# Dummy matmuls before the first operands, a split first load, a shorter LayerNorm chain and a last store in two parts

## The chip, the core and the metric

The kernel runs on one core of a Trainium2 chip. The core has five engines that work side by side, each through its own list of instructions in order: TensorE (PE in the profile, with the weight loads apart as PEld), VectorE (DVE), ScalarE (ACT), GpSimd (POOL) and SyncE (SP). SP mostly starts transfers (DMA) between main memory and the on-chip memory; ACT and POOL can start some too. Engines wait for one another and for transfers through semaphores. The metric is the device time of one execution in microseconds (us); the median of several executions is compared.

## What is computed

One decoder block on x of shape 2048 x 1024, float32:

```python
proj = x @ w_in[l] + b_in[l]                      # 1024 -> 9216 columns
q, k, v, g_attn, u_lru, g_lru, gate_logits = jnp.split(proj, SPLIT_POINTS, axis=-1)
...
y_a = attn @ w_attn_proj[l]                       # dilated window attention, three groups of 8 heads
...
y_b = (h * jax.nn.silu(g_lru)) @ w_lru_proj[l]    # convolution, gated linear recurrence over positions
gates = jax.nn.sigmoid(gate_logits).reshape(B, S, N_BRANCHES, D)
merged = gates[:, :, 0] * y_a + gates[:, :, 1] * y_b
out = merged @ w_out[l] + b_out[l]
x = layer_norm(DEEPNORM_ALPHA * x + out, ln_gain[l], ln_bias[l])
```

`layer_norm` subtracts the mean of each row of 1024, multiplies by 1/sqrt(variance + 1e-5), then by a gain, and adds a bias.

## The kernel before

Every float32 matrix product is done in three matmuls: each operand is split into a high part (rounded on ScalarE by a copy, `hi_lo` and `prep_w`) and a low part (the remainder, subtracted on VectorE or GpSimd), and high x high, high x low and low x high are added up in one bank (L597).

**Stage 1** is the input projection. It goes over half the positions at a time (two chunks of 512 columns), and in each half over 36 pairs of weight tiles. Each pair after the first of a half is done with seven products of sums of blocks in place of eight; the first pair (`order is None`) does the eight plain ones, since only loaded blocks are ready. A block of x, such as B11, is four tiles of 128 x 512 (B11: first half of the features, chunk 0; B21: second half, chunk 0; B12 and B22: the same of chunk 1). One product is twelve matmuls of 512 columns: over the four tiles, three each. The first pair multiplies A11 with B11, A12 with B21, A21 with B11, A22 with B21, then the same four weights with B12 and B22. The sums of blocks that later pairs need (T1 to T4) are formed on VectorE from the raw tiles (`comb`, `comb4`, `comb_part`). The order on each engine is the order in which the program text issues the instructions (`manual_schedule`); small tables of budgets (`left`, `Ask`) decide when a chain of follow-up work may go on.

At the very start the program issues, on SP: the weight A11, the four tiles of B11, the weight A12, B21, the weights A21 and A22, B12 and B22 (L858 to L868). Each transfer is 256 KB. ACT first issues the loads of `b72` (128 x 72 values, 288 bytes a row) and `lr` (128 x 64 values, L73 and L78), which nothing needs until `consts` (L847 to L851). There are eight semaphores for transfers, given out in turn; a transfer that gets one in use waits, before it is issued, for the earlier transfer on it to land. ScalarE converts in the order A11, B11, A12, B21, A21, B12, A22, B22; VectorE makes the low parts in the same order, with `consts` between B21 and A21.

Raw tiles, converted weights and results of stage 1 share 32 slots of 2 KB a partition; `take` hands out the slot that has been free longest and `give` puts it back at the end of the list. The memory of these slots is later covered by the tiles of stage 2.

**Stage 2** is attention (L931 to L1148), **stage 3** the projections of both branches and the merge, and **stage 4** (`out_job`, L1375 to L1425) the output product with LayerNorm, for 16 tiles of 128 rows. In `out_job` the 1024 output columns come in two matmul banks of 512 (in the last tile one of 512 and two of 256, `parts`). VectorE adds them to the scaled x (L1399), takes statistics (L1402, L1405); ScalarE takes the square root (L1406); VectorE subtracts the mean and multiplies by the gain (`centre`, L1410), makes the reciprocal (L1414) and improves it by one Newton step (L1416 to L1419: r <- r * (1.5 - 0.5 * (variance + eps) * r * r)), multiplies by it and adds the bias (L1423). Each half of 512 columns is then stored; in the last tile the first half by SP, the second by ACT.

Of the kernel before, what the change touches and what calls it, by code (L numbers as in the profile page):

```python
# [8 lines left out]
F32 = mybir.dt.float32  # L9
F32R = mybir.dt.float32r  # L10
AF = mybir.ActivationFunctionType
ALU = mybir.AluOpType
# [3 lines left out]
P = 128  # L16
S = 2048
D = 1024
KT = 8
NCH = 4  # L20
CH = 512
# [10 lines left out]
def hybrid_block_kernel(ctx: ExitStack, tc: tile.TileContext, a: dict, out: bass.AP):  # L32
    nc = tc.nc
    sp, act, dve, pool, pe = nc.sync, nc.scalar, nc.vector, nc.gpsimd, nc.tensor
# [35 lines left out]
    pool.affine_select(out=mask[:, P:256], in_=mask[:, P:256], pattern=[[-1, P]],  # L70
                       compare_op=ALU.is_ge, fill=NEG, base=0, channel_multiplier=1)
    b72 = cst.tile([P, 72], F32, name="b72")
    act.dma_start(b72, a["b_in"])  # L73
    bh = cst.tile([P, 72], F32, name="bh")
    bn = cst.tile([P, 72], F32, name="bn")
    bq = cst.tile([P, 64], F32, name="bq")
    lr = cst.tile([P, 8, 8], F32, name="lr")
    act.dma_start(lr, a["lru_vec"])  # L78
    brh = cst.tile([P, 2, 8], F32, name="brh")
    sp2 = cst.tile([P, 8], F32, name="sp2")  # L80

# [42 lines left out]
    ps = stA.enter_context(tc.tile_pool(name="ps", bufs=2, space=PSUM))  # L124
# [5 lines left out]
    def take(name, dt=F32R):  # L130
        if not vacant:
            raise RuntimeError(f"no slot at {now['n']}: {[x[1].name if hasattr(x[1],'name') else x[1] for x in home.values()]} chains {len(chains)}")
        i = vacant.pop(0)
        t = sl_p.tile([P, CH], dt, tag=f"s{i}", name=name)
        home[id(t)] = (i, t)
        return t

    def give(*ts):
        for t in ts:
            vacant.append(home.pop(id(t))[0])  # L140
# [63 lines left out]
        act.activation(t[:, 0], src, AF.Copy)  # L204
        eng.tensor_tensor(out=t[:, 1], in0=src, in1=flat(t[:, 0]), op=ALU.subtract)  # L205

    def load_raw(b, c, kk, use=""):
        kx = kk + (4 if b[1] == "2" else 0)
        r = xr[use + b, kk] = take(f"x{use}{b}{c}{kk}", F32)
        sp.dma_start(r, a["xT"][:, kx, c * CH:(c + 1) * CH])  # L210

    def drop_raw(b, kk):
        give(xr.pop((b, kk)))
# [7 lines left out]
    def load_w(s, n):  # L221
        r = raw[s, n] = take(f"w{n}_{s}", F32)
        sp.dma_start(r.rearrange("p (k f) -> p k f", f=P), w_part(s, "A21" if n[0] == "S" else n))

    def w_part(s, n):

        f = plan[s][1][int(n[1]) - 1][0]
        k = 4 * (int(n[2]) - 1)
        return a["w_in"][f, :, k:k + 4, :]
# [456 lines left out]
    def keep_raw(b, c, kk):  # L686
        load_raw(b, c, kk, "c")
# [167 lines left out]

    sp2n = cst.tile([P, 8], F32, name="sp2n")
    left.update(PE=0.0, ACT=0.0, DVE=0.0, POOL=0.0)
    load_w(0, "A11")  # L858
    for kk in K4:
        keep_raw("B11", 0, kk)  # L860
    load_w(0, "A12")
    for kk in K4:
        keep_raw("B21", 0, kk)
# [433 lines left out]
    for n in range(32):  # L1297
        c, f = divmod(n, 8)
# [63 lines left out]
    def load_xr(tt):  # L1362
        XR[tt] = vx_p.tile([P, D], F32, tag="x", name=f"x{tt}", bufs=3)
        sp.dma_start(XR[tt], a["x"][tt * P:(tt + 1) * P, :])

    def split_m(tt, ks=slice(0, 8)):
        c, b = divmod(tt, 4)
        m = ME[c][:, ks, b * P:(b + 1) * P]
        if ks.start == 0:
            MS[tt] = tuple(vx_p.tile([P, 8, P], F32R, tag=t, name=f"{t}{tt}", bufs=2) for t in ("mh", "ml"))  # L1370
        mh, ml = (t[:, ks] for t in MS[tt])
        act.activation(mh, m, AF.Copy)
        dve.tensor_tensor(out=ml, in0=m, in1=flat(mh), op=ALU.subtract)  # L1373

    def out_job(tt):  # L1375
        rows = slice(tt * P, (tt + 1) * P)
        x = XR.pop(tt)
        mh, ml = MS.pop(tt)
        last = tt == 15
        parts = [slice(0, CH), slice(CH, CH + 256), slice(CH + 256, D)] if last else [slice(0, CH), slice(CH, D)]  # L1380
        zz = [fp.tile([P, CH], F32, tag="z", name=f"z{tt}{n}", bufs=3)[:, 0:hs.stop - hs.start] for n, hs in enumerate(parts)]
        for k0, k1 in ((0, 6), (6, 8)) if tt == 0 else ((0, 8),) if tt % 4 else ((0, 7), (7, 8)):
            for z, hs in zip(zz, parts):
                for k in range(k0, k1):
                    w = WO[k]
                    pe.matmul(z, mh[:, k], w[:, 0, hs], start=(k == 0), stop=False)  # L1386
                    pe.matmul(z, mh[:, k], w[:, 1, hs], start=False, stop=False)  # L1387
                    pe.matmul(z, ml[:, k], w[:, 0, hs], start=False, stop=(k == 7))  # L1388
        if tt + 1 < 16:
            load_xr(tt + 1)  # L1390
            split_m(tt + 1, slice(0, 8 if (tt + 1) % 4 else 7))
        if tt == 1:
            for fn in at1:
                fn()
        dve.scalar_tensor_tensor(out=x, in0=x, scalar=ALPHA, in1=vec[0], op0=ALU.mult, op1=ALU.add)
        st_ = cst.tile([P, 4, 6], F32, tag="st", name=f"st{tt}", bufs=2)
        n = 0
        for z, hs in zip(zz, parts):
            dve.tensor_tensor(out=x[:, hs], in0=x[:, hs], in1=z, op=ALU.add)  # L1399
            step = 256 if last else CH  # L1400
            for q in range(hs.start, hs.stop, step):
                dve.bn_stats(out=st_[:, n, :], in_=x[:, q:q + step])  # L1402
                n += 1
        mv = cst.tile([P, 4], F32, tag="mv", name=f"mv{tt}", bufs=2)
        dve.bn_aggr(out=mv[:, 0:2], in_=st_[:, 0:n])  # L1405
        act.activation(mv[:, 2:3], mv[:, 1:2], AF.Sqrt, bias=epst)  # L1406
        halves = (slice(0, CH), slice(CH, D))

        def centre(hs):
            dve.scalar_tensor_tensor(out=x[:, hs], in0=x[:, hs], scalar=mv[:, 0:1], in1=vec[1][:, hs],  # L1410
                                     op0=ALU.subtract, op1=ALU.mult)

        centre(halves[0])
        dve.reciprocal(out=mv[:, 2:3], in_=mv[:, 2:3])  # L1414

        dve.tensor_scalar(out=mv[:, 1:2], in0=mv[:, 1:2], scalar1=EPS, scalar2=-0.5, op0=ALU.add, op1=ALU.mult)  # L1416
        dve.tensor_tensor(out=mv[:, 3:4], in0=mv[:, 2:3], in1=mv[:, 2:3], op=ALU.mult)
        dve.tensor_scalar(out=mv[:, 3:4], in0=mv[:, 3:4], scalar1=mv[:, 1:2], scalar2=1.5, op0=ALU.mult, op1=ALU.add)
        dve.tensor_tensor(out=mv[:, 2:3], in0=mv[:, 2:3], in1=mv[:, 3:4], op=ALU.mult)  # L1419
        for hs, eng in zip(halves, (sp, act) if last else (act, act)):  # L1420
            if hs.start:
                centre(hs)
            dve.scalar_tensor_tensor(out=x[:, hs], in0=x[:, hs], scalar=mv[:, 2:3], in1=vec[2][:, hs],  # L1423
                                     op0=ALU.mult, op1=ALU.add)
            eng.dma_start(out[rows, hs], x[:, hs])  # L1425
# [26 lines left out]
    for tt in range(16):  # L1452
        c, b = divmod(tt, 4)
        run(late)
        out_job(tt)
        if c + 1 < NCH:
            for f in (((0, 1), (2, 3), (4, 5, 6), (7,)) if c else ((), (0, 1, 2), (3, 4, 5, 6), (7,)))[b]:
                ya_job(8 * (c + 1) + f)
            if b == 3:
                split_m(tt + 1, slice(7, 8))  # L1460
                bring_at(c + 2)
        now["n"] += 1
# [59 lines left out]
```

## Time and profile before

| | us |
|---|---|
| median of three runs (2135.4 to 2137.36) | 2137.27 |
| the profiled execution | 2143.06 |
| its span, first to last instruction | 2141.3 |
| TensorE busy | 2101.0 |
| first matmul starts | 5.75 |
| last matmul ends | 2133.2 |

The profile is of one execution, which took longer than the three timed ones. Its mean granted TensorE clock is 0.996 of full speed. A timeline row gives the start, the duration, the engine (with a q: its queue, which issues transfers), the line, the operation with output <- inputs, and in brackets how long the engine had been idle and what ended that. Such rows can merge several instructions (x3). In a table by stage the numbers behind a stretch are the busy time and count of each engine. In the names, `xcB` are raw tiles of x blocks, `xB` the converted ones, `xT` the converted sums, `wA` raw weights, `hA` and `l` their high and low parts.

### The profile page before, as it was taken

The numbers are of one execution on the slowest core, as the hardware profiler recorded it, in microseconds if no ns is written. First come the engines' busy times: TensorE is split into PE (matmuls) and PEld (weight loads), VectorE is DVE, ScalarE is ACT, GpSimd is POOL, SyncE is SP. The second block draws the span as 40 slices with busy tenths as digits, with TensorE's granted clock in tenths as the row PEclk, the third lists the DMA queues.
The fourth block names the chain that finished last, engine by engine and source line by source line (L and its number), as shares of the span: only waits on it lengthen the run. The fifth ranks groups of instructions, "written<-read, shape, count | busy, mean of one in ns | idle before, by whom it ended". The sixth has DMA issues, their size and how long they took to land.

```text
span 2141.3 us, 36029 instructions
## 1 busy us (share of the span) xinstructions
PE 2101.0 (98%) x12016; PEld 1749.0 (82%) x12016; DVE 1700.2 (79%) x3009; ACT 1080.3 (50%) x2284; POOL 736.5 (34%) x581
## 2 busy tenths in 40 slices
PE   8999999999999999999999999999999999999998
PEld 6888887888888788888888887888888888878887
DVE  8788988999979977787787886886999645466667
ACT  6354545457446565546557666557999411121100
POOL 1545454554654312121222221222535434322120
PEclk9999999999999999999999999999999999999999
DMA  8888887998998977777778788779898788874431
GB/s 269 257 261 251 255 255 224 270 280 245 286 270 251 302 228 203 227 221 218 248 244 276 254 260 253 241 229 373 303 305 254 219 275 280 283 251 160 165 108 69
DMA packets 348266, 525.74 MB, mean 246 GB/s; under 512 B 123568, under 2 KB 156336, under 8 KB 344240
## 3 DMA queue, kind: packets, MB, share of 16 engines
q1 hardware_dynamic: 330368, 491.64, 71.0%
q0 software_dynamic: 10080, 18.35, 5.4%
q10 hardware_dynamic: 7632, 13.44, 1.8%
q8 instruction: 96, 1.57, 0.3%
q14 instruction: 90, 0.74, 0.1%
HBM read 318.18 MB, written 190.45 MB: 238 GB/s over the span
## 4 chain that ended last, share of the span: by engine, by line
PE 82%; ACT 6%; DMA 5%; DVE 5%; issue 1%; SPq 1%; POOL 0%; DVEq 0%; ACTq 0%; POOLq 0%
PE q L597 59%; ACT p L991 4%; PE z L1388 3%; PE z L1386 3%; PE z L1387 3%; PE yb L1276 2%; PE yb L1277 2%; PE yb L1278 2%; PE o L1029 1%; PE ya L1354 1%; PE ya L1355 1%; PE ya L1356 1%; PE vtp L348 1%; ACT ptb L1014 1%; DMA yb_scr<-gB 1%
## 5 line engine op out<-in xcount | busy, mean ns | idle before, releaser
L597 PE MATMUL q<-xT,hS 128*128 128x512 f32 x1680 | 519.0, 390 | 0.4 <-DVE y L216 0.4
L597 PE MATMUL q<-xT,l 128*128 128x512 f32 x1120 | 436.0, 389 | 0.0
L597 PE MATMUL q<-xB,hA 128*128 128x512 f32 x1248 | 389.0, 393 | 6.0 <-ACT xB L204 5.7
L597 PEld LDWEIGHTS q<-xT,hS 128*128 128x128 f32 x1680 | 314.1, 188 | 65.4 <-issue 0.8
L597 PE MATMUL q<-xB,l 128*128 128x512 f32 x904 | 354.8, 392 | 1.9 <-DMA l<-wl_scr 1.8
L597 PEld LDWEIGHTS q<-xB,hA 128*128 128x128 f32 x1248 | 235.0, 189 | 56.1 <-ACT xB L204 5.7
L597 PEld LDWEIGHTS q<-xT,l 128*128 128x128 f32 x1120 | 210.2, 188 | 44.0
L597 PEld LDWEIGHTS q<-xB,l 128*128 128x128 f32 x904 | 171.1, 189 | 39.4 <-DMA l<-wl_scr 2.7
L216 POOL TENSOR_TENSOR S<-S,wA 128x512 f32<-128x512 f32 x35 | 45.7, 1305 | 418.9 <-DVE S L216 328.4
L216 POOL TENSOR_TENSOR sw<-sw,sin 128x512 f32<-128x512 f32 x96 | 160.7, 1679 | 72.0 <-DMA sw<-y 59.4
L261 ACT ACTIVATE hA<-wA 128x512 fp32r<-128x512 f32 x218 | 135.7, 624 | 90.3 <-DMA wA<-in_w_in_dram 43.0
L597 PE MATMUL q<-xB,hS 128*128 128x512 f32 x560 | 175.6, 395 | 3.0 <-DVE v L216 3.0
L991 ACT ACTIVATE p<-p,sta 128x256 f32<-128x256 f32 (+1 forms) x384 | 172.2, 455 | 5.9 <-DVE sta L983 5.2
L597 PE MATMUL q<-xT,hA 128*128 128x512 f32 x560 | 173.0, 390 | 1.5 <-DVE xT L205 0.9
L261 ACT ACTIVATE hS<-S 128x512 fp32r<-128x512 f32 x175 | 109.1, 623 | 99.2 <-DVE S L216 54.6
L216 POOL TENSOR_TENSOR l<-wA,hA 128x512 fp32r<-128x512 f32 x68 | 104.9, 1543 | 83.0 <-ACT hA L261 66.5
L597 PEld LDWEIGHTS q<-xB,hS 128*128 128x128 f32 x560 | 105.1, 190 | 25.0 <-issue 3.8
L597 PEld LDWEIGHTS q<-xT,hA 128*128 128x128 f32 x560 | 104.8, 188 | 24.6 <-DVE xT L205 1.3
L983 DVE CUSTOM_DVE_ANT_0 p<-s,mask 128x256 f32<-128x256 f32 (+1 forms) x384 | 118.7, 360 | 4.7 <-PE s L976 3.7
L216 DVE TENSOR_TENSOR y<-y,cos 128x512 f32<-128x512 f32 x96 | 108.8, 1139 | 14.8 <-DMA sw<-y 14.6
L1360 POOL TENSOR_TENSOR me<-gA,ybr 128x512 f32<-128x512 f32 x32 | 49.9, 1573 | 181.2 <-DVE gA L1359 119.6
L1388 PE MATMUL z<-wo,ml 128*128 128x512 f32 (+1 forms) x264 | 101.2, 383 | 0.9 <-DVE ml L1373 0.8
(201 smaller groups left out, 4423.7 us busy)
## 6 DMA issues: line engine op xcount, KB each, us to landing
wA<-in_w_in_dram SPq DMA_DIRECT2D x253, 256.0 KB, 5.0
wl_scr<-l SPq DMA_DIRECT2D x105, 512.0 KB, 4.9
l<-wl_scr SPq DMA_DIRECT2D x105, 512.0 KB, 4.8
sw<-y SPq DMA_DIRECT2D x384, 64.0 KB, 3.0
wS<-in_w_in_dram SPq DMA_DIRECT2D x70, 256.0 KB, 4.5
wS<-in_w_in_dram POOLq DMA_DIRECT2D x70, 256.0 KB, 6.3
qh_scr<-hi SPq DMA_DIRECT2D x48, 256.0 KB, 5.2
v_scr<-vs SPq DMA_DIRECT2D x48, 256.0 KB, 4.4
```

The source lines that it names most:

```text
L216: eng.tensor_tensor(out=out, in0=in0, in1=in1, op=op)
L261: act.activation(h, r, AF.Copy)
L597: pe.matmul(bank, w[:, ks], x[:, kk, xx], start=(first and i == 0), stop=(last and i == 11))
L983: dve.tensor_tensor_reduce(out=st["p", i, j][:, h, lo:256], in0=st["s", i, j // 2][h][:, j % 2, lo:256], in1=mask[:, lo:256], scale=1.0, s ...
L991: act.activation(p, p, AF.Exp, scale=-1.0, bias=s[:, h:h + 1], accum_out=s[:, 2 + h:3 + h])
L1276: pe.matmul(yb, WL[f][:, 0, k], xx[:, 0], start=(k == 0), stop=False)
L1277: pe.matmul(yb, WL[f][:, 0, k], xx[:, 1], start=False, stop=False)
L1278: pe.matmul(yb, WL[f][:, 1, k], xx[:, 0], start=False, stop=(k == 7))
L1360: pool.tensor_tensor(out=ME[c][:, f], in0=ga, in1=yb, op=ALU.add)
L1386: pe.matmul(z, mh[:, k], w[:, 0, hs], start=(k == 0), stop=False)
L1387: pe.matmul(z, mh[:, k], w[:, 1, hs], start=False, stop=False)
L1388: pe.matmul(z, ml[:, k], w[:, 0, hs], start=False, stop=(k == 7))
```

## The change

Four edits: five matmuls on a zeroed tile ahead of everything on TensorE; tiles 0 and 2 of B11 are loaded through ACT's queue, and `b72` and `lr` behind them; the Newton step in two operations in place of three; the second half of the last row tile is normalised and stored in two parts of 256 columns.

```diff
-    act.dma_start(b72, a["b_in"])
...
-    act.dma_start(lr, a["lru_vec"])
...
-    def load_raw(b, c, kk, use=""):
+    def load_raw(b, c, kk, use="", eng=sp):
         kx = kk + (4 if b[1] == "2" else 0)
         r = xr[use + b, kk] = take(f"x{use}{b}{c}{kk}", F32)
-        sp.dma_start(r, a["xT"][:, kx, c * CH:(c + 1) * CH])
+        eng.dma_start(r, a["xT"][:, kx, c * CH:(c + 1) * CH])
...
     left.update(PE=0.0, ACT=0.0, DVE=0.0, POOL=0.0)
+    warm = take("warm", F32)
+    dve.memset(warm[:, 0:256], 0.0)
+    wps = ps.tile([P, CH], F32, tag="g", name="wps", bufs=2)
+    for _ in range(5):
+        pe.matmul(wps[:, 0:256], warm[:, 0:P], warm[:, 0:256], start=True, stop=True)
+    give(warm)
     load_w(0, "A11")
     for kk in K4:
-        keep_raw("B11", 0, kk)
+        load_raw("B11", 0, kk, "c", sp if kk % 2 else act)
+    act.dma_start(b72, a["b_in"])
+    act.dma_start(lr, a["lru_vec"])
     load_w(0, "A12")
...
-        halves = (slice(0, CH), slice(CH, D))
+        halves = parts
...
-        dve.tensor_tensor(out=mv[:, 3:4], in0=mv[:, 2:3], in1=mv[:, 2:3], op=ALU.mult)
-        dve.tensor_scalar(out=mv[:, 3:4], in0=mv[:, 3:4], scalar1=mv[:, 1:2], scalar2=1.5, op0=ALU.mult, op1=ALU.add)
-        dve.tensor_tensor(out=mv[:, 2:3], in0=mv[:, 2:3], in1=mv[:, 3:4], op=ALU.mult)
-        for hs, eng in zip(halves, (sp, act) if last else (act, act)):
+        dve.scalar_tensor_tensor(out=mv[:, 3:4], in0=mv[:, 2:3], scalar=mv[:, 2:3], in1=mv[:, 1:2], op0=ALU.mult, op1=ALU.mult)
+        dve.tensor_scalar(out=mv[:, 2:3], in0=mv[:, 3:4], scalar1=1.5, scalar2=mv[:, 2:3], op0=ALU.add, op1=ALU.mult)
+        for hs, eng in zip(halves, (sp, act, sp) if last else (act, act)):
```

The dummy tile takes the first slot and gives it back, so every later tile of stage 1 lies one slot further on. The matmuls, and all other work up to LayerNorm, stand in the same order as before on every engine.

The start of SP's list before (`xcB1100` is tile 0 of B11, chunk 0; DMAHW and a digit is a transfer semaphore):

```order
L223 DMA wA11_0_226<-in_w_in_dram 128x512
L210 DMA xcB1100_228<-in_xT_dram 128x512
L210 DMA xcB1101_230<-in_xT_dram 128x512
L210 DMA xcB1102_232<-in_xT_dram 128x512
L210 DMA xcB1103_234<-in_xT_dram 128x512
L223 DMA wA12_0_236<-in_w_in_dram 128x512
L210 DMA xcB2100_238<-in_xT_dram 128x512 [waits DMAHW0_49]
L210 DMA xcB2101_240<-in_xT_dram 128x512 [waits DMAHW1_49]
```

SP issues all four tiles of B11, and B21's first tile waits for the transfer that has semaphore 0, which is `b72`. The start of ACT's list in the changed kernel:

```order
L208 DMA xcB1100_234<-in_xT_dram 128x512
L208 DMA xcB1102_238<-in_xT_dram 128x512
L865 DMA b72_193<-in_b_in_dram 128x72
L866 DMA lr_197<-in_lru_vec_dram 128x64
L259 ACT_TABLE_LOAD
L259 ACTIVATE hA11_0_274<-wA11_0_232 128x512 [waits DMAHW1_49]
L202 ACTIVATE xB11_278<-xcB1100_234 128x512 [waits DMAHW0_49]
L202 ACTIVATE xB11_278<-xcB1101_236 128x512 [waits DMAHW3_49]
```

Tiles 0 and 2 now stand at the head of ACT's list, the two small loads behind them, and semaphore 0 belongs to tile 0. The end of VectorE's list in the changed kernel, from the reciprocal of the last row tile on:

```order
L1420 RECIPROCAL mv15_22719<-mv15_22719 128x1 [waits Activation_49]
L1422 TENSOR_SCALAR mv15_22719<-mv15_22719 128x1
L1423 SCALAR_TENSOR_TENSOR mv15_22719<-mv15_22719 128x1 [waits DVE_49]
L1424 TENSOR_SCALAR mv15_22719<-mv15_22719 128x1 [waits DVE_49]
L1428 SCALAR_TENSOR_TENSOR x15_22610<-x15_22610,mv15_22719,vec2_21021 128x512 [waits DVE_49]
L1416 SCALAR_TENSOR_TENSOR x15_22610<-x15_22610,mv15_22719,vec1_21019 128x256
L1428 SCALAR_TENSOR_TENSOR x15_22610<-x15_22610,mv15_22719,vec2_21021 128x256 [waits DVE_49]
L1416 SCALAR_TENSOR_TENSOR x15_22610<-x15_22610,mv15_22719,vec1_21019 128x256
L1428 SCALAR_TENSOR_TENSOR x15_22610<-x15_22610,mv15_22719,vec2_21021 128x256 [waits DVE_49]
```

Three small operations stood between L1416 and the first multiplication before, and one pair of 512 columns where two pairs of 256 stand now.

## The prediction

> **What bounds the kernel now.** I read the page's first two parts, then the timeline of both ends, the waits of TensorE, and windows by stage.
>
> ```profile
> PE 2101.0 (98%) x12016; PEld 1749.0 (82%) x12016; DVE 1700.2 (79%) x3009; ACT 1080.3 (50%) x2284; POOL 736.5 (34%) x581
> PE 82%; ACT 6%; DMA 5%; DVE 5%; issue 1%; SPq 1%; POOL 0%; DVEq 0%; ACTq 0%; POOLq 0%
> ```
>
> TensorE is the bound: 98% busy, 82% of the chain of waits. An edit pays only if the matmuls that come after it start earlier, or if it lies behind the last one. The change touches the first 20 us and the last 3 of a span of 2141.3 us. The start, from the timeline (start, duration, engine, in brackets the idle time before and who ended it):
>
> ```profile
> 0.81 0.41 ACTq L73 DMA_DIRECT2D b<-in_b_in_dram  x1
> 1.24 1.84 SPq L210 DMA_DIRECT2D xcB<-in_xT_dram  x4
> 4.20 0.63 ACT L261 ACTIVATE hA<-wA 128x512 fp32r<-128x512 f32 x1 [1.19 <-DMA wA<-in_w_in_dram]
> 4.86 0.69 DVE L216 TENSOR_TENSOR l<-wA,hA 128x512 fp32r<-128x512 f32 x1 [3.89 <-ACT hA L261]
> 5.06 1.98 ACT L204 ACTIVATE xB<-xcB 128x512 fp32r<-128x512 f32 x3 [0.23 <-DMA xcB<-in_xT_dram]
> 5.75 1.52 PE L597 MATMUL q<-xB,hA 128*128 128x512 f32 x2 [5.75 <-ACT xB L204]
> 7.92 0.63 ACT L204 ACTIVATE xB<-xcB 128x512 fp32r<-128x512 f32 x1 [0.88 <-DMA xcB<-in_xT_dram]
> 13.28 2.66 ACT L204 ACTIVATE xB<-xcB 128x512 fp32r<-128x512 f32 x4 [0.72 <-DMA xcB<-in_xT_dram]
> 16.52 0.73 PE L597 MATMUL q<-xB,hA 128*128 128x512 f32 x2
> 16.59 0.68 DVE L216 TENSOR_TENSOR l<-wA,hA 128x512 fp32r<-128x512 f32 x1
> 17.33 0.50 PE L597 MATMUL q<-xB,l 128*128 128x512 f32 x1
> 17.59 2.50 DVE L205 TENSOR_TENSOR xB<-xcB,xB 128x512 fp32r<-128x512 f32 x4 [0.32 <-ACT xB L204]
> 48.23 0.50 PE L597 MATMUL q<-xT,hA 128*128 128x512 f32 x1 [0.91 <-DVE xT L205]
> ```
>
> The first matmul starts at 5.75. Three gates follow: block B12 (the four conversions at 13.28 wait for their loads), the rest of the fourth weight (l at 16.59, ending 17.27, for the matmul at 17.33), and at 48.23 VectorE's splits, which TensorE waits for 0.91 us. In between:
>
> ```profile
> 5.70:10.30 4.60, 4.55 (x10) 3.38 (x11) 3.75 (x6) 3.54 (x6) 0.00 (x0) 1.00 1.01 365
> 10.30:14.90 4.60, 4.60 (x21) 3.68 (x21) 4.58 (x14) 3.66 (x7) 0.00 (x0) 1.00 1.05 392
> 17.30:47.30 30.00, 29.97 (x131) 24.51 (x131) 29.36 (x45) 19.69 (x36) 5.97 (x6) 1.00 0.84 234
> ```
>
> After the stretch come busy times and counts of PE, PEld, DVE, ACT and POOL, the granted clock, DMA share and GB/s. The first 4.6 us hold 10 matmuls, the next 21 in the same time: the array begins at half pace, though the clock column says 1.00 in both. From 17.3 to 47.3 VectorE is busy 29.36 of 30.00 us: it sets when 48.23 happens. DMA moves 365 to 392 GB/s in the first two stretches: loading bounds the start.
>
> **Dummy matmuls.** They wait for a new memset of 256 columns behind one_t on VectorE, idle then until 4.86.
>
> ```profile
> 13.10 0.23 DVE L852 MEMSET ubs<- 128x200 f32 x1
> L1029 PE MATMUL o<-ptb,V 128*64 128x128 f32 x1200 | 77.1, 279 | 14.4 <-ACT ptb L1014 13.9
> 1521.60 1.97 PE L1029 MATMUL o<-ptb,V 128*64 128x128 f32 x32 [0.24 <-ACT ptb L1014]
> ```
>
> The nearest memset (200 columns) takes 0.23, so TensorE begins at about 1.3. The trace has no plain float32 matmul of 256 columns. The nearest is L1029: 600 in the program leave 1200 records, and 32 records of 128 columns take 1.97 us, 0.062 each. Five dummies are ten records of 256 columns: 1.2 us at full pace, 2.5 at half; twice that, 4.9, if the two halves of L1029, which write different partitions, overlap. So they end between 3.8 and 6.2; the first operands come near 5.5 if tile 0 is there when the weight's conversion ends (4.83 + 0.66), and real work is delayed by 0 to 0.7 us.
>
> What can they gain? At full pace the stretch from 5.75 to 10.3 would save half of itself, about 2.3 us, but the matmuls would then wait for the same data. TensorE waits already: the matmul at 16.52 starts where the conversion of the fourth weight hands over, and the next one waits for l until 17.33. That conversion stands in ScalarE's order behind B12, which waits for DMA. Even a TensorE that arrives later has the 0.91 at 48.23 to spare. **I take 0**; the bounds are a gain of 2.3 (no cover) and a loss of 0.
>
> On this the Trainium skill, "TensorE: Matmul & The Clock Gate", Part 1, says that the array starts at half clock and is released after about 3.4 us of sustained activity. The trace agrees on the pace. By that rule alone the answer is the 2.3 us gain, which is a rival below.
>
> **Two queues for the first x, small loads behind them.** Tile 0 is issued on ACT at 0.81 in place of behind the weight at 1.24; SP has two issues fewer before the next weight. B21's first load waited for b_in; now it waits for x tile 0, which should land at about the same time. ScalarE issues four in place of two, so it is free 0.8 later, and it idles 1.19 before 4.20. What decides is bytes, from the DMA view of 0 to 10 us in 40 slices:
>
> ```profile
> SPq L210 <- DMA b<-in_b_in_dram: 0.8, 1, 0.8
> DMA  0000000399747999999999997899999999999999
> GB/s 0 0 0 0 0 0 0 123 207 203 146 103 184 303 363 374 320 396 400 393 418 369 320 295 303 336 369 369 369 360 393 385 393 369 344 336 385 401 402 385
> ```
>
> From 1.75 to 4.0 it moves 223 GB/s on average against some 390 later; with the dip at 5.5 to 6.5 (314) that is 0.45 MB missing, 1.2 us. The edit can recover at most that, since as many bytes lie ahead of B12 as before; at least 0, as the same engines serve both queues. **I take 0.5**: near 2.5 the engines are busy at half rate, where 288-byte rows share them with the weight, and that half should go; the time to the first byte at 1.75 stays. B12, its conversions and VectorE's queue from 17.59 all move by it, so does 48.23, and behind that TensorE runs on: 0.5 off the end.
>
> The Trainium skill, "DMA: Bandwidth & Descriptors", section "Issuing engines are not separate DMA queues", says that issuing from several engines saves only the sequencer's time. By that, tile 0 gains 1.24 - 0.81 = 0.43 and the sum would be 0.4 in place of 0.5.
>
> **LayerNorm and the last store.** In 15 of 16 rows the small operations lie under matmuls:
>
> ```profile
> 2032.00:2076.00 44.00, 44.00 (x196) 36.44 (x195) 33.80 (x56) 3.87 (x6) 9.35 (x6) 1.00 0.39 132
> ```
>
> TensorE has no gap there and VectorE is idle 10 of 44 us: worth 0. Were that cover gone, 16 times 0.2. The last row stands bare:
>
> ```profile
> 2135.29 0.16 DVE L1417 TENSOR_TENSOR mv<-mv 128x1 f32<-128x1 f32 x1
> 2135.49 0.21 DVE L1418 TENSOR_SCALAR mv<-mv 128x1 f32<-128x1 f32 x1
> 2135.74 0.16 DVE L1419 TENSOR_TENSOR mv<-mv 128x1 f32<-128x1 f32 x1
> 2135.93 0.75 DVE L1423 SCALAR_TENSOR_TENSOR x<-x,mv,vec 128x512 f32<-128x512 f32 x1
> 2136.60 0.75 DVE L1410 SCALAR_TENSOR_TENSOR x<-x,mv,vec 128x512 f32<-128x512 f32 x1
> 2137.38 0.75 DVE L1423 SCALAR_TENSOR_TENSOR x<-x,mv,vec 128x512 f32<-128x512 f32 x1
> 2138.16 0.34 ACTq L1425 DMA_DIRECT2D out_dram<-x  x1
> L1399 DVE TENSOR_TENSOR x<-x,z 128x256 f32<-128x256 f32 x2 | 0.8, 412 | 1.9 <-PE z L1388 1.9
> L1399 DVE TENSOR_TENSOR x<-x,z 128x512 f32<-128x512 f32 x1 | 0.7, 689 | 0.1
> out_dram<-x ACTq DMA_DIRECT2D x1, 256.0 KB, 2.0
> ```
>
> Three operations take 0.64 from start to start (2135.29 to 2135.93); two like L1418, each 0.25 to its successor, make 0.50; between 0.1 and 0.25 less, I take 0.15. The half row: one pair takes 2136.60 to 2138.13. A 256-column operation is 0.28 shorter (412 against 689 ns), so starts step by 0.50 to a dependent and 0.39 to an independent successor (0.78 and 0.67 now): 0.50 + 0.39 + 0.50 + 0.47 = 1.86 against 1.53, **0.33 later**. The last transfer is 128 KB in place of 256; at 390 GB/s that is **0.34 less** of its 2.0; 0.1 if the 2.0 is mostly fixed. The middle part leaves on ACT 0.9 earlier and is out of its way; SP's first part was issued at 2136.71. Tail: 0.15 - 0.33 + 0.34 = 0.15 gained, bounds 0.25 gained and 0.15 lost.
>
> **Sum.** 0 + 0.5 + 0.15 = 0.65 us off. Against the profiled execution (2143.06, 1.76 of it around the span) that gives 2142.4; against the median of the three runs, 2137.27, it gives **2136.6**. Terms at their bounds: 2133.5 to 2137.4. A measurement of this kernel tells about 0.2%, 4.3 us, from no change: no bound reaches it.
>
> **Rivals.** What can be larger are later waits that move with the start:
>
> ```profile
> 331.93 1.19 PE L597 MATMUL q<-xB,hS 128*128 128x512 f32 x2 [2.67 <-DVE v L216]
> 332.00:338.00 6.00, 6.00 (x16) 4.81 (x17) 5.93 (x9) 1.75 (x3) 1.97 (x2) 0.50 0.92 189
> 1306.95 0.50 PE L597 MATMUL q<-xB,l 128*128 128x512 f32 x1 [1.78 <-DMA l<-wl_scr]
> 1307.97 0.63 PE L597 MATMUL q<-xB,l 128*128 128x512 f32 x1
> 1310.93 0.63 PE L597 MATMUL q<-xT,hS 128*128 128x512 f32 x2
> ```
>
> A wait of 2.67 is followed by 6 us at clock 0.50: 2.67 + 3.0 = 5.7 us. That is close to the 5.8 by which the profiled run lies above the median, so the timed runs may lack it. The wait before 1306.95 is followed by 0.63 us matmuls too, until 1310.93: 1.8 + half of 4.0 = 3.8.
> - *A new stall (slower).* If VectorE's queue near 329 comes late in the changed kernel's timed runs as in this profile, TensorE loses the 5.7: 2136.6 + 5.7 = 2142.3. It decides once the wait is long enough for the clock to fall: 1.78 was, the 0.91 at 48.23 was not. For it: the profile has one. Against it: order and work are unchanged after the start, and a shift of all engines alike moves no wait. 0.08.
> - *A stall goes (faster).* The load that 1306.95 waits for comes in time: 2136.6 - 3.8 = 2132.8, less with a further one. For and against it the same. 0.12.
> - *The dummies pay in full.* If the data lead and pace decides, 2.3 more: 2134.3. For it, 10 matmuls in 4.6 us; against it, the waits at 16.52, 17.33 and 48.23. 0.10.
> - *The change does not do what it says*: the dummies end too early to hold the pace, or tile 0 lands with the weight, no sooner; both leave 2137.1 and no visible difference. 0.15.
>
> **Numbers.** My forecast has the remaining 0.55. Faster by over 0.2% (below 2133.0): most of the second rival and a sliver of the third, 0.12. Slower (above 2141.5): the first, 0.08. Within: 0.80. The likeliest case alone spans 2133.5 to 2138.4 (the bounds above, and at the top half of the 2.0 us between the three runs). For 8 in 10 I reach past the missing stall, and half way to the new one: 2132.0 to 2139.8.
>
> **What would show it.** Right: dummies from about 1.3, the full pace by 8, and yet the fourth weight's l still ends TensorE's wait near 16.8; B12's conversions near 12.8; 48.23 at 47.7; the last store issued 0.2 later but landing earlier. Wrong: TensorE without a wait at 16 to 17 or 48 and 2 us earlier; B12 unmoved; a wait over 1.5 us with a clock of 0.50 at a place that had none. More than 4 us either way would mean that I misread the first 48 us or that the later stalls decide.

## The result and the profile after

| | before | changed |
|---|---|---|
| median (14 executions of each) | 2135.11 us | 2141.63 us |
| lowest, highest | 2130.93, 2139.46 | 2136.43, 2143.42 |
| ratio of changed to before | | 1.0027, 95% interval 1.0018 to 1.0036 |
| a second comparison (12 and 35 executions) | 2134.17 us | 2138.59 us, ratio 1.0020, 1.0011 to 1.0028 |

The ratios are of the means. The changed kernel is slower, by 5.8 us in the first comparison (0.0027 x 2135) and 4.3 in the second. 2136.6 was forecast, with 2139.8 as the upper end. One caution on the traces: the profiled execution of the changed kernel (2136.43) is the fastest of its 14, and the one of before (2143.06) is slower than all of its 14. So the two spans, 2134.6 and 2141.3, stand the wrong way round, and only stretches between the same two events can be compared.

**The start.** Timeline of the changed kernel:

```profile
1.32 4.28 PE L860 MATMUL wps<-warm 128*128 128x256 f32 x10 [1.32 <-DVE warm L857]
4.97 0.63 ACT L259 ACTIVATE hA<-wA 128x512 fp32r<-128x512 f32 x1 [0.99 <-DMA wA<-in_w_in_dram]
6.18 0.50 PE L595 MATMUL q<-xB,hA 128*128 128x512 f32 x1 [0.58 <-ACT xB L202]
7.33 0.40 PE L595 MATMUL q<-xB,l 128*128 128x512 f32 x1
7.57 0.63 PE L595 MATMUL q<-xB,hA 128*128 128x512 f32 x2
13.76 2.67 ACT L202 ACTIVATE xB<-xcB 128x512 fp32r<-128x512 f32 x4 [0.96 <-DMA xcB<-in_xT_dram]
17.80 0.50 PE L595 MATMUL q<-xB,l 128*128 128x512 f32 x1
48.70 0.50 PE L595 MATMUL q<-xT,hA 128*128 128x512 f32 x1 [0.91 <-DVE xT L203]
```

Its DMA view of 0 to 10 us, in 40 slices:

```profile
GB/s 0 0 0 0 0 0 0 74 90 229 279 303 221 254 303 303 328 401 410 393 393 410 399 366 382 387 380 264 300 281 200 213 295 344 328 369 393 393 393 361
```

Read each timeline row against its counterpart in the prediction. The dummies run 1.32 to 5.60, and the real matmuls go at full pace from 7.33 on (the next starts 0.24 later). But the first weight arrives later (its conversion at 4.97, before 4.20), so do the first matmul (6.18, before 5.75), block B12 (13.76, before 13.28) and the gate of VectorE's splits (48.70, before 48.23), which still waits 0.91. Between these two traces the start lost 0.47 us where 0.5 was to be gained.

**The tail.** The last row tile of the changed kernel, from the reciprocal on; then its last transfer in the DMA view (size, median us from issue to landing); then the reciprocal of the kernel before:

```profile
2128.53 0.16 DVE L1420 RECIPROCAL mv<-mv 128x1 f32<-128x1 f32 x1
2128.77 0.22 DVE L1423 SCALAR_TENSOR_TENSOR mv<-mv 128x1 f32<-128x1 f32 x1
2129.27 0.75 DVE L1428 SCALAR_TENSOR_TENSOR x<-x,mv,vec 128x512 f32<-128x512 f32 x1
2129.94 0.48 DVE L1416 SCALAR_TENSOR_TENSOR x<-x,mv,vec 128x256 f32<-128x256 f32 x1
2131.37 0.48 DVE L1428 SCALAR_TENSOR_TENSOR x<-x,mv,vec 128x256 f32<-128x256 f32 x1
```

```profile
out_dram<-x SPq DMA_DIRECT2D x1, 128.0 KB, 1.7
```

```profile
2135.10 0.16 DVE L1414 RECIPROCAL mv<-mv 128x1 f32<-128x1 f32 x1
```

From the reciprocal to the end of the span it is 6.07 us (2134.6 - 2128.53), before 6.20: 0.13 gained.

**A wait that was not there.** TensorE's waits in the changed kernel have a new second place, and the timeline shows it at the border between stage 1 and stage 2. The view of waits (sum, times, longest):

```profile
PE s L982 <- DVE sta L989: 4.8, 2, 4.5
```

The chain of waits (start, duration, who):

```profile
1462.03 8.18 DMA mg_scr<-y
```

The timeline, and the window of the 10 us behind it (the last three numbers are clock, DMA share and GB/s):

```profile
1462.03 0.33 ACTq L374 DMA_DIRECT2D mg_scr<-y  x1
1470.33 0.56 DVE L1022 COPY ptb<-pt 128x384 f32<-128x384 f32 x1 [4.94 <-DMA mg_scr<-y]
1471.97 1.99 PE L982 MATMUL s<-B,A 64*128 64x256 f32 x12 [4.50 <-DVE sta L989]
1503.89 0.42 DVE L1022 COPY ptb<-pt 128x256 f32<-128x256 f32 x1
```

```profile
1470.00:1480.00 10.00, 7.97 (x124) 7.55 (x126) 8.50 (x36) 9.71 (x37) 0.25 (x1) 0.69 1.02 413
```

The same two views of the kernel before:

```profile
1467.68 0.33 ACTq L376 DMA_DIRECT2D mg_scr<-y  x1
1471.84 0.56 DVE L1016 COPY ptb<-pt 128x384 f32<-128x384 f32 x1
1473.48 1.32 PE L976 MATMUL s<-B,A 64*128 64x256 f32 x12 [0.27 <-DVE sta L983]
1507.33 0.42 DVE L1016 COPY ptb<-pt 128x256 f32<-128x256 f32 x1
```

```profile
1470.00:1480.00 10.00, 8.52 (x121) 7.17 (x122) 8.27 (x40) 10.00 (x38) 2.77 (x3) 0.91 1.03 409
```

`ptb` is the buffer into which attention copies its transposed probabilities. Before, the first copy starts 4.16 us after the last result `y` of stage 1 went off to main memory, and waits for nothing. In the changed kernel it waits until that store has landed, 8.18 us after its issue, since the DMA engines are full (share 1.02). VectorE and ScalarE, which shares these copies, stand, so TensorE stands for 4.50 us, and its clock is 0.69 over the next 10 us. The last row of each timeline is the 22nd copy on VectorE: 41.86 us after the store's issue (1503.89 - 1462.03), before 39.65.

Why does a copy of stage 2 wait for a store of stage 1? `ptb` lies where the slots of stage 1 lay. The dummy tile was taken from the front of the list of 32 slots and given back at its end, which moved each later tile by one place; the first `ptb` came to lie over the last `y`. In the built programs the last `y` ends at byte 150208 of its partitions before and at 152256 in the changed kernel, and the first `ptb` starts at 152000 in both, so in the changed kernel they overlap by 256 bytes. The list of instructions says what follows from it, with the semaphore of a transfer (DMAHW5, that of the last store) in the changed kernel's first copy, on ScalarE, and none in that of before:

```
L1014 ACTIVATE ptb_14477<-pt_14463 128x6x64 [waits PE_49]
L1020 ACTIVATE ptb_14485<-pt_14471 128x6x64 [waits DMAHW5_49,PE_49]
```

### The profile page after: what moved, and what is told of

It reads as the page before. It is cut to its first block, busy times and chain, and to the rows that moved or that the text cites. A ratio compares the mean times of both kernels' runs of the same rounds, so it can differ in the third digit from the quotient of the medians.

```text
span 2134.6 us, 36038 instructions
## 1 busy us (share of the span) xinstructions
PE 2097.5 (98%) x12026; PEld 1748.0 (82%) x12026; DVE 1697.4 (80%) x2996; ACT 1080.2 (51%) x2284; POOL 736.7 (35%) x581
## 4 chain that ended last, share of the span: by engine, by line
PE 64%; ACT 6%; DVE 4%; DMA 2%; issue 1%; SPq 1%; POOL 0%; DVEq 0%; ACTq 0%; POOLq 0%
PE q L595 38%; ACT p L997 4%; PE yb L1282 3%; PE yb L1283 3%; PE z L1392 3%; PE yb L1284 3%; PE z L1394 3%; PE z L1393 3%; PE o L1035 2%; PE ya L1360 1%; PE ya L1361 1%; PE ya L1362 1%; ACT ptb L1020 1%; PE s L982 1%; DMA mg_scr<-y 1%
## 5 line engine op out<-in xcount | busy, mean ns | idle before, releaser
L214 DVE TENSOR_TENSOR y<-y,cos 128x512 f32<-128x512 f32 x96 | 102.6, 1074 | 15.7 <-DMA sw<-y 15.6
L1393 PE MATMUL z<-wo,mh 128*128 128x512 f32 (+1 forms) x264 | 101.0, 383 | 0.0
```

The source lines that it names most:

```text
L214: eng.tensor_tensor(out=out, in0=in0, in1=in1, op=op)
```

## The experiments

Theory S: the slots moved by one are the cause. Theory Q: the new loading of x is, with its semaphores. Theory R: stalls that vary from run to run. A later doubt was whether the dummies themselves cost something (D).

**1. All edits, the dummy tile not from the slots** (e1_own_tile).

```diff
-    warm = take("warm", F32)
+    warm = ub_free[0]
...
-    give(warm)
```

> The changed kernel, but the zeroed tile of the dummy matmuls is one of the three ub buffers, not one taken from the 32 slots; so every later tile of stage 1 lies in the slot where it lay before the change. All four edits are kept otherwise. Theory S (the slots moved on by one, so the first ptb tile of attention lies over a tile whose last store has not landed): the wait of some 4.5 us near 1467 to 1472 goes, and the time falls to that of the kernel before plus the direct terms, +0.47 at the start and -0.12 at the tail: ratio about 1.0002. Theory Q (the split load of x is the cause of all of it): nothing changes against the changed kernel, ratio 1.0027. Theory R (stalls that vary from run to run): ratio anywhere, and the wait at 1467 to 1472 stays or goes without the time following it.

Measured: 2136.94 us median against 2135.17; ratio 1.0009 (0.9999 to 1.0020). The wait is gone:

```profile
1462.92 0.33 ACTq L374 DMA_DIRECT2D mg_scr<-y  x1
1466.34 0.56 DVE L1021 COPY ptb<-pt 128x384 f32<-128x384 f32 x1
1502.27 0.42 DVE L1021 COPY ptb<-pt 128x256 f32<-128x256 f32 x1
```

The first copy comes 3.42 us after the store, the 22nd after 39.35. The first ratio of the changed kernel, 1.0027, lies outside the interval, and the second, 1.0020, at its edge: Q is unlikely as the whole explanation, and experiment 6 settles it.

**2. The kernel before, the slots moved by one, no instruction added** (e2_rotate_only).

```diff
+    give(take("turn0", F32))
     load_w(0, "A11")
```

> The kernel before, with one slot taken and given back ahead of the first load and no instruction added or moved. Theory S: the stall at the end of stage 1 appears as in the changed kernel (VectorE and ScalarE at the ptb copy wait 3 to 5 us for the store of a y tile, TensorE then waits over 4 us and its clock falls below 0.8), and the time rises by 4 to 7 us: ratio 1.002 to 1.003. Theories Q and R: the same instructions take the same time, ratio 1.0000 within 0.1%.

Measured: 2139.18 against 2135.17; ratio 1.0016 (1.0006 to 1.0026). A line that issues nothing makes the kernel slower, by less than the 1.002 to 1.003 that S gave (the interval reaches them), and the stall is there:

```profile
1460.63 0.33 ACTq L376 DMA_DIRECT2D mg_scr<-y  x1
1468.70 0.56 DVE L1017 COPY ptb<-pt 128x384 f32<-128x384 f32 x1 [3.98 <-DMA mg_scr<-y]
1470.35 1.99 PE L977 MATMUL s<-B,A 64*128 64x256 f32 x12 [4.17 <-DVE sta L984]
1502.80 0.42 DVE L1017 COPY ptb<-pt 128x256 f32<-128x256 f32 x1
```

42.17 us from the store to the 22nd copy. Q and R had nothing here.

**3 and 4. One edit at a time** (e3_loads_only: the load edit; e4_tail_only: LayerNorm and the last store).

```diff
-    act.dma_start(b72, a["b_in"])
-    act.dma_start(lr, a["lru_vec"])
...
-        keep_raw("B11", 0, kk)
+        load_raw("B11", 0, kk, "c", sp if kk % 2 else act)
+    act.dma_start(b72, a["b_in"])
+    act.dma_start(lr, a["lru_vec"])
```

> The kernel before with the load edit alone: tiles 0 and 2 of the first x block through ScalarE's queue, b72 and lr behind them. Theory S: only the start moves, the first weight lands some 0.7 us later, block B12 is converted from about 13.76 in place of 13.28 and the matmul at 48.23 starts near 48.7: +0.5 us, ratio 1.0002. Theory Q: the later start is what costs the 5 us, by waits that come later for loads that moved: ratio 1.0025. Without a wait in TensorE at 1467 in either.

```diff
-        halves = (slice(0, CH), slice(CH, D))
+        halves = parts
...
-        for hs, eng in zip(halves, (sp, act) if last else (act, act)):
+        for hs, eng in zip(halves, (sp, act, sp) if last else (act, act)):
```

(and the Newton step as in the change)

> The kernel before with the LayerNorm and last-store edits alone. All theories: 0.1 to 0.15 us off the time between the last bn_aggr and the end (7.16 before), ratio 0.9999; the small operations of the 15 earlier rows show nothing. A ratio of 1.001 or more would mean that the fused operations delay a row under the matmuls, which none of the theories has.

Measured: the loads 1.0002 (0.9992 to 1.0013), with the weight and the gate as late as in the changed kernel; the tail 0.9999 (0.9988 to 1.0010), 6.10 us from the reciprocal (2126.80) to the end of its span (2132.9). The loads, with the weight's conversion and the gate:

```profile
4.87 0.63 ACT L259 ACTIVATE hA<-wA 128x512 fp32r<-128x512 f32 x1 [0.90 <-DMA wA<-in_w_in_dram]
48.82 0.50 PE L595 MATMUL q<-xT,hA 128*128 128x512 f32 x1 [0.93 <-DVE xT L203]
```

**5. The dummies alone** (e5_dummies_only): the kernel before with the memset and five matmuls, on `ub_free[0]`.

```diff
+    warm = ub_free[0]
+    dve.memset(warm[:, 0:256], 0.0)
+    wps = ps.tile([P, CH], F32, tag="g", name="wps", bufs=2)
+    for _ in range(5):
+        pe.matmul(wps[:, 0:256], warm[:, 0:P], warm[:, 0:256], start=True, stop=True)
```

> The kernel before with the five dummy matmuls alone, on a ub buffer, so that no slot moves. Theory S: the array runs at full pace from the first real matmul, which saves nothing since the matmul at 48.23 waits for VectorE all the same: within 0.3 us of before at 48.23, ratio 1.0000. Rival D (the dummies cost something later, since they draw on the same clock allowance: the changed kernel stands some 3 us above the sum of its traced parts, 0.6 at the start + 2.5 at the end of stage 1 - 0.1): ratio 1.001 or more.

Measured: ratio 1.0005 (0.9995 to 1.0015): no gain, and no cost that could be told; the 1.001 of D is not excluded. The gate comes 0.33 us later than before, just outside the 0.3 that was expected.

```profile
13.62 2.67 ACT L204 ACTIVATE xB<-xcB 128x512 fp32r<-128x512 f32 x4 [0.72 <-DMA xcB<-in_xT_dram]
48.56 0.50 PE L597 MATMUL q<-xT,hA 128*128 128x512 f32 x1 [0.91 <-DVE xT L205]
```

The gate follows block B12 by 34.94 us (48.56 - 13.62), as in the kernel before (48.23 - 13.28 = 34.95) and in the changed one (34.94), whatever the pace of the first matmuls.

**6. All edits, the slots moved by twelve** (e6_turn_twelve).

```diff
     give(warm)
+    for j in range(11):
+        give(take(f"turn{j}", F32))
```

> The changed kernel with all its edits, and the slots moved on by eleven more (twelve in all), by taking and giving back without an instruction. The first ptb tile then waits for no transfer; the second waits for one, 6 us after the last store's issue. Theory S, which has it that the place of the slots is the cause and not the dummies or the loads: from the issue of the last store of stage 1 to the 22nd ptb copy on VectorE it takes 39.4 to 39.7 us, as in the kernels that are not moved (41.9 to 42.2 in those moved by one), and the ratio falls from 1.0027 to about 1.0005. Theories Q and R: the ratio stays at 1.002 to 1.003.

Measured: 2133.99 against 2134.17; ratio 0.9998 (0.9988 to 1.0007). Dummies, loads and tail are all in it, the dummy tile is still a slot, and the loss is gone:

```profile
1462.49 0.33 ACTq L374 DMA_DIRECT2D mg_scr<-y  x1
1465.90 0.56 DVE L1024 COPY ptb<-pt 128x384 f32<-128x384 f32 x1
1501.88 0.42 DVE L1024 COPY ptb<-pt 128x256 f32<-128x256 f32 x1
```

39.39 us to the 22nd copy.

**7. Half of the load edit** (e7_small_behind): `b72` and `lr` behind the first block, all of x on SP.

```diff
-    act.dma_start(b72, a["b_in"])
-    act.dma_start(lr, a["lru_vec"])
...
         keep_raw("B11", 0, kk)
+    sp.dma_start(b72, a["b_in"])
+    sp.dma_start(lr, a["lru_vec"])
```

> The kernel before, with b72 and lr taken off ScalarE's queue and issued by SP behind the four tiles of the first block; all x tiles stay on SP. It is the half of the load edit on which the prediction's 0.5 us rested (no 288-byte rows beside the first weight). If that half was right: the first weight lands some 0.3 to 0.5 us before 4.2, and block B12 and the matmul at 48.23 follow it. If what holds things up is that b72 and lr, wherever they are issued late, keep the semaphores that the next weight and B12's first tile need: the weight lands a little earlier, B12 does not, and 48.23 stays or comes later by up to 0.6. Ratio 0.9998 or 1.0002; the times of the start are read from the trace.

Measured: ratio 0.9994 (0.9986 to 1.0003).

```profile
3.81 0.63 ACT L259 ACTIVATE hA<-wA 128x512 fp32r<-128x512 f32 x1 [1.73 <-DMA wA<-in_w_in_dram]
13.51 2.67 ACT L202 ACTIVATE xB<-xcB 128x512 fp32r<-128x512 f32 x4 [0.99 <-DMA xcB<-in_xT_dram]
48.46 0.50 PE L595 MATMUL q<-xT,hA 128*128 128x512 f32 x1 [0.91 <-DVE xT L203]
```

The weight lands 0.39 earlier (3.81 against 4.20), as both readings had it, but B12 does not follow (13.51 against 13.28): an earlier first weight was worth nothing at 48.23 in this trace. Experiment 6 has the reverse: its first conversion is the latest of all (5.94, behind a 1.28 us table load on ScalarE), and its B12 is the earliest with the load edit (13.12).

**8. The changed kernel again** (e8_changed_again), no edit.

> The changed kernel as it is, on the chip of the three others. Theory S: the same 41.9 us from the last store to the 22nd ptb copy, a wait of 4.5 us, ratio 1.0014 to 1.0027 (its traced parts sum to 3.0 us, the first comparison gave 5.8 with an interval of 3.8 to 7.7). Theory R: a wait at the end of stage 1 of another size, as the stalls near 329 and 1305 us vary.

Measured: ratio 1.0020 (1.0011 to 1.0028). TensorE waits 4.39 us at the same place, after 4.50 and, in experiment 2, 4.17, which is not the varying stall of theory R:

```profile
1473.82 1.99 PE L982 MATMUL s<-B,A 64*128 64x256 f32 x12 [4.39 <-DVE sta L989]
```

**9. Another dose** (e9_turn_seven): the kernel before, the slots moved by seven.

```diff
+    for j in range(7):
+        give(take(f"turn{j}", F32))
     load_w(0, "A11")
```

> The kernel before with the slots moved on by seven, no instruction added. The second ptb tile, not the first, then waits for the transfer on the semaphore of the last store. Theory S: VectorE's second ptb copy, which comes 6.0 us after the issue of that store in the kernels that do not wait, comes when the store has landed, after 8.1 to 8.3 us; the first copy stays at 3.4 to 4.2. About 2 us of wait in place of 4.5, so from the store to the 22nd copy between 39.6 and 41.5 us. Theories Q and R: the second copy stays near 6.0 and the 22nd near 39.5.

```profile
1463.28 0.33 ACTq L376 DMA_DIRECT2D mg_scr<-y  x1
1467.44 0.56 DVE L1023 COPY ptb<-pt 128x384 f32<-128x384 f32 x1
1471.53 0.69 DVE L1023 COPY ptb<-pt 128x512 f32<-128x512 f32 x1 [2.16 <-DMA mg_scr<-y]
1472.63 2.06 PE L1008 MATMUL pt<-ident,p 64*128 64x64 f32 x16 [1.73 <-ACT p L998]
1504.70 0.42 DVE L1023 COPY ptb<-pt 128x256 f32<-128x256 f32 x1
```

```profile
1470.00:1480.00 10.00, 7.62 (x92) 6.50 (x90) 5.75 (x23) 7.46 (x27) 0.00 (x0) 0.66 1.01 405
```

As theory S has it (timeline and window), the wait moved to the second copy, which comes 8.25 us after the store, and it is 2.16 us long; the 22nd comes after 41.42. With one execution (2137.36) its time says little.

**10. What may be had** (e10_behind_and_tail): the kernel before with experiment 7's edit and the LayerNorm and last-store edits.

> The kernel before with b72 and lr on SP behind the first block (as in e7_small_behind, 0.9994) and with the LayerNorm and last-store edits (0.1 us), without dummies and without a second queue for x; no slot moves. If e7's 0.9994 was an effect: 0.9993, and clearly below 1. If it was chance, since the start of block B12 did not move there: 0.9999, and the only sure gain is the 0.1 us between the last reciprocal and the end.

Measured: 2134.10 against 2134.86; ratio 0.9994 (0.9985 to 1.0003). It beats the changed kernel, whose intervals lie above 1.001. That it beats the kernel before is not shown: both kernels with these loads came out at 0.9994, but with B12 at 13.51 and 13.32 their start is no earlier.

**11. Two queues, small loads first** (e11_two_queues_small_first).

```diff
+    act.dma_start(b72, a["b_in"])
+    act.dma_start(lr, a["lru_vec"])
     load_w(0, "A11")
     for kk in K4:
-        keep_raw("B11", 0, kk)
+        load_raw("B11", 0, kk, "c", sp if kk % 2 else act)
```

> The kernel before with tiles 0 and 2 of the first block on ScalarE's queue, but behind b72 and lr, which stay first there. If it is the second queue that slows the first weight (its transfer shares the engines with an x tile issued at the same time): the tile is now issued near 1.7, so the weight lands as before, conversion near 4.2 to 4.6. If it is the late b72 and lr: the same here, since they are early again, but block B12's conversions come at 13.0 to 13.3 and not later. Where both hold, 48.23 is found again; a weight at 4.9 and B12 at 13.8 would show that neither is the cause.

```profile
4.24 0.63 ACT L259 ACTIVATE hA<-wA 128x512 fp32r<-128x512 f32 x1 [0.27 <-DMA wA<-in_w_in_dram]
48.25 0.50 PE L595 MATMUL q<-xT,hA 128*128 128x512 f32 x1 [0.75 <-DVE xT L203]
```

Weight and gate are where they were before the change. This speaks against the second queue as such, and for an x tile issued at the same time as the weight, or for the small loads behind it. The run changes both back at once and does not part them; and it is one trace, where B12 scatters by 0.6 us between kernels with the same loads.

**All traces at the border.** Worked out from the rows of each trace: time from the issue of the last store to VectorE's first, second and 22nd `ptb` copy, and the clock of 1470 to 1480 us.

| kernel | slots moved | 1st | 2nd | 22nd | clock |
|---|---|---|---|---|---|
| before | 0 | 4.16 | 6.01 | 39.65 | 0.91 |
| loads only (3) | 0 | 4.16 | 6.01 | 39.65 | 0.83 |
| tail only (4) | 0 | 4.16 | 6.01 | 39.60 | 0.83 |
| small behind (7) | 0 | 4.17 | 6.02 | 38.31 | 1.00 |
| behind and tail (10) | 0 | 4.17 | 6.02 | 38.32 | 1.00 |
| two queues, small first (11) | 0 | 4.16 | 6.01 | 38.29 | 1.00 |
| own tile (1) | 0 | 3.42 | 5.26 | 39.35 | 0.83 |
| dummies only (5) | 0 | 3.42 | 5.27 | 39.54 | 0.83 |
| turned by twelve (6) | 12 | 3.41 | 5.26 | 39.39 | 0.83 |
| turned by seven (9) | 7 | 4.16 | 8.25 | 41.42 | 0.66 |
| turned by one (2) | 1 | 8.07 | 9.92 | 42.17 | 0.71 |
| changed | 1 | 8.30 | 10.14 | 41.86 | 0.69 |
| changed again (8) | 1 | 8.19 | 10.04 | 42.24 | 0.66 |

The window of the clock is fixed in time while the border moves with each run (the last store is issued at 1460.6 to 1467.7), so part of a fall can lie outside it; in the kernel before, some of it does. The kernels that collide take 41.4 to 42.2, the others 38.3 to 39.7. Moved by one, the border costs between 2.2 us (41.86 - 39.65) and 3.9 (42.24 - 38.31). Moves by 1 and 7 collide, those by 0 and 12 do not: it was luck of the place, too, that the kernel before had no collision. The timed executions say the same: the two ratios of the changed kernel average 1.0023, those of all edits without the collision (1 and 6) 1.0003; the difference is 0.0020, or 4.3 us, give or take about 2 by their intervals. Much of it stands in TensorE's granted clock: its mean over the timed executions is 0.9966, 0.9967 and 0.9969 in the three comparisons of a kernel moved by one, and 0.9976 to 0.9983 in all others of twelve executions or more, the kernel before among them. Experiments 2 and 8 lie 0.0012 and 0.0016 below their kernel before; if TensorE sets the time throughout, that is, as an upper estimate, 2.6 and 3.4 us of 2135.

What the clock does there shows in windows of 0.5 us. It reads 1.00 or 0.50, but for the windows in which it changes: at 0.50 it stays 3.4 us in the kernels with 0.83 and in the kernel before (1478.15 to 1481.56), 6.8 us in all four traces with a collision (1469.42 to 1476.24 in the changed kernel), and not at all in experiments 7, 10 and 11. The changed kernel's window:

```profile
1469.50:1476.00 6.50, 3.97 (x47) 3.72 (x49) 5.06 (x22) 5.71 (x21) 0.00 (x0) 0.50 1.01 410
```

So a collision brings a wait and 6.8 us at half clock, part of it while TensorE waits anyway; a kernel without one has 3.4 us at half clock or none, and the cost of the border depends on which of the two it is compared with.

## Why the prediction was wrong, step by step

- **What bounds the kernel: right.** The gates that the forecast named for the first 48 us, and the bare chain of the last row, are those of the new trace.
- **Dummies, "I take 0": right** for what they were meant to do. The pace was full from 7.33 on, the matmul that needs l(A22) still came late (17.80), and 48.23 followed B12 by the same 34.9 us. So the rival that they pay in full fell. In experiment 6, where TensorE stood for 1.24 us after the dummies, the pace was half again from 9.2 to 12.6, and B12 was no later for it. What they cost came by another way, below.
- **Two queues, "I take 0.5": not gained, and likely lost.** The step that failed: "near 2.5 the engines are busy at half rate ... and that half should go". It did not go. Adding up the slices (0.25 us each) to 4.0 us gives 0.50 MB before (2006 x 0.25) and 0.51 MB after (2056 x 0.25): the same bytes, now shared by the weight and an x tile, and the weight, which is needed first, came 0.77 later. Its conversion starts at 4.61 to 4.97 in four traces with the load edit and at 4.14 to 4.58 in five without; that the sharing is the reason was not tested alone. The step behind it, that an earlier start moves B12, is not borne out either (experiment 7). B12 starts at 13.03 to 13.62 in five traces without the load edit (before, 2, 4, 5, 9) and at 13.12 to 13.86 in five with it (changed, 1, 3, 6, 8); the means are 13.3 and 13.6. So the term is some 0.3 lost, within a scatter of 0.6 to 0.7, and not 0.5 gained. The Trainium skill, "DMA: Bandwidth & Descriptors", section "Issuing engines are not separate DMA queues", says that transfers of several engines run on the same DMA engines; the bytes agree, but the 0.43 us of issue time that was worked out from it was not gained.
- **LayerNorm and last store, 0.15: right,** 0.13 in the trace and 0.10 in experiment 4. Two operations take 0.50 for 0.64 (2128.77 to 2129.27), the two narrow pairs 1.91 for 1.53 (2129.94 to 2131.85; 1.86 was forecast), the last landing 1.7 for 2.0.
- **The rival of a new stall: right in kind, wrong in place and in its chance.** It was put near 329 us and given 0.08, with the argument: "order and work are unchanged after the start, and a shift of all engines alike moves no wait". That is the step that lost the prediction. The order was unchanged; the memory was not. The description of the change even says that each later tile lies one slot further on, and no term of the sum was given to it. The sign that was named as proof of error, a wait over 1.5 us with a clock of 0.50 at a place that had none, is what the trace shows (4.50 us).
- **The old stalls: misread.** The forecast took the wait of 2.67 at 331.93 for something that the timed runs may lack, and thought that a wait long enough makes the clock fall. All thirteen traces have that wait (2.55 to 2.67), the changed kernel's too:

```profile
330.86 0.70 PE L595 MATMUL q<-xB,hS 128*128 128x512 f32 x2 [2.55 <-DVE v L214]
```

  What varies is the clock behind it: 6.8 us at 0.50 in the kernel before, 3.4 in ten traces, none in the changed kernel and in experiment 11. The 1.78 us before 1306.95, on which the rival *A stall goes* rests, are in the trace of the kernel before alone; the longest wait of the twelve others there is 0.6. The two together are one reason why the profiled spans stand the wrong way round.
- **The base: luck in the number.** 2137.27 was the median of three executions; that of the 14 is 2135.11. The forecast of 2136.6 therefore stood 2.2 us too high, and on the side of the result: it missed 2141.63 by 5.0 us, and from the true base it would have missed by 7.2.

What stays open: start, border and tail sum to 0.3 + (2.2 to 3.9) - 0.1, or 2.4 to 4.1 us. The second comparison measured 4.3 (2.3 to 6.0), the first 5.8 (3.8 to 7.7). Whether the first holds a further loss of some 2 us or chance isn't settled; the runs on single edits are each too coarse for it.

## What to carry to other kernels

Where memory is handed out in turn, a temporary buffer is never without effect: it moves all that comes after it, and what a later stage lays over that memory can get other waits. So after an edit compare not only the order of the instructions but what each waits for, and for each new wait on a transfer ask when that transfer lands in a trace, not whether it was issued long ago. A change of place alone can be tried by itself, without an instruction, and should be, before an edit is judged by its time.

## What the runs showed of the hardware

- A 256 KB store was 8.18 us on its way from issue to landing with the DMA engines full (the chain above; the copies that waited for it began 8.1 to 8.3 after its issue), where the last store of the kernel before, of 256 KB too, took 2.0, and that of the changed kernel, 128 KB, 1.7.
- TensorE's clock fell without a long wait, and stayed up after one. In experiment 1 the longest wait ahead of the fall is 0.57 us, and the clock is then 0.50 for 3.4 us (the window; the timeline row is the wait in which it fell); in experiment 7, with waits as long, it stayed at 1.00 (table). The 1.3 us between 39.6 and 38.3 in the table go with it. At 331 a wait of 2.55 was followed by no fall in the changed kernel.

```profile
1472.50:1475.50 3.00, 2.55 (x24) 2.55 (x26) 0.64 (x1) 3.00 (x11) 0.00 (x0) 0.50 1.01 411
```

```profile
1472.95 3.16 PE L1034 MATMUL o<-ptb,V 128*64 128x128 f32 x28 [0.57 <-ACT ptb L1019]
```

  The Trainium skill, "TensorE: Matmul & The Clock Gate", Part 1, ties the fall in its table of states to some 3.4 us without work, and tells further on of a kernel in which short gaps between groups of matmuls were enough. By the 0.57 us here the table's figure is not needed for a fall. What decides between none, 3.4 and 6.8 us at half clock was not tried.
- At the border the time at half clock came in pieces of 3.41 us (six traces) or 6.82 (the four with a collision), or not at all (three), worked out from the windows of 0.5 us.
- Half the wait did not cost half: 2.16 us at the second copy ended 0.4 to 0.8 us short of 4 to 5 us at the first (41.42 against 41.86 to 42.24), with 6.8 us at half clock in both.
- The dummies had an effect at the border of their own. Kernels with them start the first copy 3.4 us after the store in place of 4.2 (table), as the first score matmuls no longer wait for VectorE (0.53 us for `y` in the kernel before, nothing in experiment 5); at most 0.3 us of it is left at the 22nd copy among the kernels at 0.83. That the reason is the bank `wps`, which takes a turn among the banks of stage 1, was not tested apart from the dummies.
